# A gated-MLP down projection rewritten as Strassen's product of halves, partly run between the tiles of the up projection

## The chip, the cores and the metric

One core of a Trainium2 chip runs one program. The metric is the time on the device in microseconds (us), the median of several executions. The engines are TensorE (PE: matmuls into PSUM), VectorE (DVE), ScalarE (ACT), GpSimd (POOL) and SyncE (SP), which here issues the loads. PSUM has eight banks of 128 partitions x 512 fp32.

## The reference, cut to what matters

A diffusion block: adaLN, a token mixer with four branches, then a gated MLP with a depthwise convolution, and a final RMSNorm. 512 tokens, D = 1024 channels, hidden width F = 2816. Only the last part is changed:

```python
def conv_ffn(h, p):
    u, g = jnp.split(h @ p['ffn_w_up'], 2, axis=-1)
    g = depthwise_conv(g, p['ffn_conv_w'], p['ffn_conv_b'])
    return (jax.nn.silu(g) * u) @ p['ffn_w_down']
...
x = x + gate2 * conv_ffn(ada_norm(x, norm2_g, shift2, scale2), p)
return rmsnorm(x, final_norm_g)
```

## The kernel before

All matmuls keep about fp32 precision by splitting each operand into a rounded part and a rest: `hi` is a ScalarE cast to fp32r, `lo` a VectorE subtraction, and a product is three matmuls (hi·hi, hi·lo, lo·hi; helper `mm3`). So each weight tile that is loaded costs a ScalarE pass and a VectorE pass over it (`load_split`, tags "wh" and "wl" with three slots each, "wr" with two for the raw data).

Activations are channel-major: partitions are channels, the 512 tokens lie along the free dimension. The up projection makes 44 tiles (22 of gates g, 22 of u) of 8 x 3 = 24 matmuls each, with weights stationary and 512 tokens moving (`up`, L1015). For hidden tile f the loop at L1032 makes g, convolves it (one ScalarE pass, two VectorE passes out of PSUM), applies silu, makes u, multiplies, and splits the result into `act[f]`. The down projection (L1045) then makes eight output tiles of 128 channels, each over 22 hidden chunks, the last one in two halves of 256 tokens; each tile gets the gate and the residual, its squares are added up, it is transposed on TensorE and copied to token-major `xo`. The last tile is followed by the square root, the scaling of all rows and the four output transfers.

A scheduler orders the instructions of each engine once, at build time; each engine then runs its list in order and waits on semaphores. Every operation goes through one helper, so all carry line L60; names of tiles tell them apart. In PSUM four banks have the tag "big" (up tiles `pup`, down tiles `pdn`, and others) and four the tag "ps".

Of the kernel before, what the change touches and what calls it, by code (L numbers as in the profile page):

```python
# [8 lines left out]
F32 = mybir.dt.float32  # L9
F32R = mybir.dt.float32r  # L10
AF = mybir.ActivationFunctionType
ALU = mybir.AluOpType
# [6 lines left out]
KT = 8  # L19
# [2 lines left out]
EPS = 1e-6  # L22
FH = 2816
NF = FH // P
GW = 64
RW = 63

# [12 lines left out]
INV2PI = 1.0 / (2 * math.pi)  # L40
MAGIC = 1.5 * 2.0 ** 23
PI_LO = 3.1415925
CUT = 576


@with_exitstack
def block_kernel(ctx: ExitStack, tc: tile.TileContext, A):
# [24 lines left out]
    pp = ctx.enter_context(tc.tile_pool(name="psum", bufs=1, space=bass.MemoryType.PSUM))  # L72

    def ps(name="ps"):
        big = name in ("pin", "pbr", "pup", "pdn", "pwo", "pkc", "pvc")
        return pp.tile([P, T], F32, name=name, tag="big" if big else "ps", bufs=4)


# [37 lines left out]
    def col(name, i=0, n=1):  # L116
        o = COLS[name][0] + i
        return cols[:, o:o + n]
# [4 lines left out]
    def temp(pool, tag="hm"):  # L123
        return lambda n: pool.tile([P, T], F32, name="hm", tag=tag, bufs=2)[:, :n]
# [54 lines left out]
    hxh = hp.tile([P, KT, T], F32R, name="hxh")  # L179
    hxl = hp.tile([P, KT, T], F32R, name="hxl")  # L180

    def yslot(name, shape=(P, 2, T), dt=F32R):
        return hp.tile(list(shape), dt, name=name, tag="y", bufs=8)
# [812 lines left out]
    with ExitStack() as ff:  # L996
        fp = ff.enter_context(tc.tile_pool(name="ffn", bufs=1))
        h2h, h2l = hxh, hxl

        def tmp(n):  # L1000
            return yslot("hm", dt=F32)[:, 0, :n]

        for h, hs in enumerate(halves):
            if h:
                norm2_cols(h)
                norm2_rows(h)
            for k in range(KT):
                modulate(tmp, h2h[:, k, hs], h2l[:, k, hs], xt[k][:, hs], rb2[h], a2col[:, k:k + 1], modc[:, 8 + k:9 + k])
        act = []
# [12 lines left out]

        first = {}
        for m in (NF, 0, NF + 1):
            first[m] = (load_split(A["wup"][m], name="wup"), ps("pup"))
        for hs in halves:
            for ms in ((NF, 0), (NF + 1,)):
                for k in range(KT):
                    for m in ms:
                        up_step(first[m][1], first[m][0], k, hs)  # L1030

        for f in range(NF):  # L1032
            pg = first[NF + f][1] if NF + f in first else up(NF + f)
            gt = fp.tile([P, T], F32, name="gt", tag="gt", bufs=2)
# [4 lines left out]
            act.append(yslot("act") if f < 8 else fp.tile([P, 2, T], F32R, name="act", tag=f"act{f}"))  # L1039
            split(act[f][:, 0], act[f][:, 1], gt)  # L1040


        xo = fp.tile([P, 4, D], F32, name="xo")
        tmp = temp(fp)
        for mt in range(KT):  # L1045
            ws = []
            for c in range(0, NF, KT):
                n = min(KT, NF - c)
                ws.append(load_split(A["wdn"][mt, :, c * P:(c + n) * P], n * P, name="wdn"))
            for hs in ((full,) if mt < KT - 1 else halves):  # L1050
                p = ps("pdn")[:, hs]
# [4 lines left out]
                V.scalar_tensor_tensor(xt[mt][:, hs], p, modc[:, 24 + mt:25 + mt], xt[mt][:, hs], ALU.mult, ALU.add)  # L1056
                n = hs.stop - hs.start
                if mt < KT - 1:
                    sumsq(tmp, ssq[:, hs], xt[mt][:, hs], mt == 0)
                else:  # L1060
                    sq = tmp(n)
                    S.activation(sq, xt[mt][:, hs], AF.Square)
                xg = fp.tile([P, T], F32, name="xg", tag="gt", bufs=2)[:, hs]
                V.tensor_scalar(xg, xt[mt][:, hs], col("final", mt), None, ALU.mult)
                tt = range(4)[hs.start // P:hs.stop // P]
                if mt == KT - 1:
                    r = rms_cols(sum_cols(ssq[:, hs], sq))
                pt = ps("pxt")[:, hs]
                for i in range(len(tt)):
                    PE.transpose(pt[:, i * P:(i + 1) * P], xg[:, i * P:(i + 1) * P], ident)  # L1070
                if mt == 4:
                    preload_sqrt(ssq[:, 0:1])
                if mt < KT - 1:
                    S.copy(xo[:, tt.start:tt.stop, mt * P:(mt + 1) * P], pt.rearrange("p (t c) -> p t c", c=P))
                    continue
                for i, t in enumerate(tt):
                    rt = r[:, i:i + 1]
                    V.tensor_scalar(xo[:, t, :CUT], xo[:, t, :CUT], rt, None, ALU.mult)
                    S.mul(xo[:, t, CUT:mt * P], xo[:, t, CUT:mt * P], rt)
# [55 lines left out]
def _arrays(x, c, ctx, c_ctx, w_mod, b_mod, norm1_g, norm2_g, w_in, pool_w, pool_scale,  # L1135
# [78 lines left out]
```

## Time and profile before

| | |
|---|---|
| median of 3 runs | 856.35 us (856.13 to 857.44) |
| profiled execution, its own time | 855.23 us |
| its span in the trace | 853.4 us |
| TensorE busy | 832.1 us, 97% of the span |
| VectorE busy | 502.6 us, 59% |
| ScalarE busy | 332.1 us, 39% |
| up projection, first to last tile | about 475.6 to 717.8 us |
| down projection | 717.8 to 843.4 us |
| after the last matmul of the down projection | about 10 us |

Busy shares are averages over stages; what a stage is bound by is read from its own stretch. Matmul rows overlap their neighbours, so their durations can't be added up; the distance between starts counts.

### The profile page before, as it was taken

The page shows a single profiled execution, that of the slowest core. Times are in us where ns is not written, and L with a number is a line of the kernel's source. Part 1 is how long each engine was busy: PE and PEld are TensorE (multiplying, and loading weights), DVE is VectorE, ACT ScalarE, POOL GpSimd, SP SyncE. Part 2 cuts the span into 40 slices and gives each one's busy share as a digit, 9 for nine tenths or more (in the row PEclk, how much of TensorE's full clock was granted, in tenths as well). Part 3 has the DMA queues.
Part 4 walks back from the last instruction along what each step waited for, and adds up shares of the span by engine and source line. Part 5 has one row for each costly group of instructions (what it writes and reads, how often), then busy time and mean ns, then how long its engine had stood idle before and what let it go on. Part 6 is the DMA issues. An engine that isn't in the chain of part 4 may idle for free.

```text
span 853.4 us, 10736 instructions
## 1 busy us (share of the span) xinstructions
PE 832.1 (97%) x4192; PEld 683.8 (80%) x4192; DVE 502.6 (59%) x874; ACT 332.1 (39%) x519; POOL 5.9 (1%) x16
## 2 busy tenths in 40 slices
PE   6999999989999999999999999999999999999995
PEld 2577888868888888888889988888888888888885
DVE  4879998699797863445444964444444444232333
ACT  6634452625454332323333453333333333222321
POOL 0100000000000000000000000000000000000000
PEclk9999999999999999999999999999999999999998
DMA  8912314645656542223332233222222333332312
GB/s 315 414 60 74 99 44 140 190 144 208 210 166 220 185 158 93 93 93 130 113 122 76 74 124 99 98 97 92 91 96 95 99 99 93 87 107 84 93 57 99
DMA packets 30363, 107.31 MB, mean 126 GB/s; under 512 B 3783, under 2 KB 4935, under 8 KB 29288
## 3 DMA queue, kind: packets, MB, share of 16 engines
q1 hardware_dynamic: 30312, 106.62, 37.6%
q8 instruction: 33, 0.54, 0.3%
q14 instruction: 18, 0.15, 0.0%
HBM read 104.51 MB, written 2.10 MB: 125 GB/s over the span
## 4 chain that ended last, share of the span: by engine, by line
PE 86%; DVE 8%; ACT 2%; DMA 1%; issue 1%; SPq 0%; DVEq 0%; ACTq 0%
PE pup L60 28%; PE pin L60 25%; PE pdn L60 14%; PE pwo L60 5%; PE pbr L60 5%; PE pss L60 1%; DVE za L60 1%; PE pKe L60 1%; PE pav L60 1%; DVE winl L60 1%; DVE zb L60 1%; PE pmod L60 1%; DMA cb<-in_crow_dram 1%; DMA wm<-in_wmB_dram 1%; DVE wgl L60 1%
## 5 line engine op out<-in xcount | busy, mean ns | idle before, releaser
L60 PE MATMUL pup<-hxh,wupl 128*128 128x512 f32 (+1 forms) x376 | 140.8, 376 | 0.0
L60 PE MATMUL pup<-hxl,wuph 128*128 128x512 f32 (+1 forms) x376 | 140.6, 376 | 0.0
L60 PE MATMUL pup<-hxh,wuph 128*128 128x512 f32 (+1 forms) x376 | 139.9, 376 | 0.7 <-ACT wuph L60 0.4
L60 PE MATMUL pdn<-act,wdnh 128*128 128x512 f32 (+1 forms) x396 | 112.7, 368 | 0.0
L60 PE MATMUL pin<-hxh,wgh 128*128 128x512 f32 x256 | 101.2, 395 | 0.6 <-ACT wgh L60 0.6
L60 PE MATMUL pin<-hxh,wgl 128*128 128x512 f32 x256 | 100.3, 392 | 0.0
L60 PE MATMUL pin<-hxl,wgh 128*128 128x512 f32 x256 | 100.2, 391 | 0.0
L60 DVE TENSOR_TENSOR wupl<-wupr,wuph 128x1024 fp32r<-128x1024 f32 x44 | 53.9, 1225 | 71.7 <-ACT wuph L60 69.8
L60 ACT CAST wuph<-wupr 128x1024 fp32r<-128x1024 f32 x44 | 46.3, 1053 | 92.6 <-PE pup L60 90.2
L60 PEld LDWEIGHTS pdn<-act,wdnh 128*128 128x128 f32 x396 | 71.6, 189 | 12.0
L60 PEld LDWEIGHTS pup<-hxh,wupl 128*128 128x128 f32 x376 | 70.7, 188 | 13.1 <-DVE wupl L60 0.2
L60 PEld LDWEIGHTS pup<-hxh,wuph 128*128 128x128 f32 x376 | 70.1, 188 | 13.7 <-ACT wuph L60 0.6
L60 PEld LDWEIGHTS pup<-hxl,wuph 128*128 128x128 f32 x376 | 70.6, 188 | 12.8
L60 PE MATMUL pdn<-act,wdnl 128*128 128x512 f32 (+1 forms) x198 | 72.4, 366 | 0.0
L60 DVE TENSOR_TENSOR wdnl<-wdnr,wdnh 128x1024 fp32r<-128x1024 f32 (+1 forms) x24 | 27.2, 1134 | 63.3 <-ACT wdnh L60 63.2
L60 ACT ACTIVATE sg<-pin 128x512 f32<-128x512 f32 x32 | 19.2, 600 | 113.5 <-PE pin L60 113.4
L60 DVE SCALAR_TENSOR_TENSOR sg<-sg,pbr 128x512 f32<-128x512 f32 x24 | 16.5, 689 | 75.8 <-PE pbr L60 75.8
L60 PEld LDWEIGHTS pin<-hxh,wgh 128*128 128x128 f32 x256 | 48.1, 188 | 10.5 <-ACT wgh L60 1.0
L60 PEld LDWEIGHTS pin<-hxh,wgl 128*128 128x128 f32 x256 | 48.1, 188 | 10.3 <-issue 0.5
L60 PEld LDWEIGHTS pin<-hxl,wgh 128*128 128x128 f32 x256 | 48.1, 188 | 9.8 <-issue 0.5
L60 ACT CAST wdnh<-wdnr 128x1024 fp32r<-128x1024 f32 (+1 forms) x24 | 23.6, 983 | 72.5 <-PE pdn L60 66.7
L60 PE MATMUL pin<-hxh,winh 128*128 128x512 f32 x128 | 51.7, 404 | 0.0
(265 smaller groups left out, 1427.5 us busy)
## 6 DMA issues: line engine op xcount, KB each, us to landing
wupr<-in_wup_dram SPq DMA_DIRECT2D x44, 512.0 KB, 3.4
wgr<-in_wg_dram SPq DMA_DIRECT2D x32, 640.0 KB, 3.9
wm<-in_wmB_dram SPq DMA_DIRECT2D x32, 512.0 KB, 4.6
wm<-in_wmA_dram SPq DMA_DIRECT2D x8, 1024.0 KB, 9.9
winr<-in_win_dram SPq DMA_DIRECT2D x16, 512.0 KB, 3.5
wdnr<-in_wdn_dram SPq DMA_DIRECT2D x16, 512.0 KB, 3.5
wor<-in_wout_dram SPq DMA_DIRECT2D x8, 512.0 KB, 3.5
wdnr<-in_wdn_dram SPq DMA_DIRECT2D x8, 384.0 KB, 3.1
```

Of the source, the lines that this page charges most:

```text
L60: ins = f(*a, **k)
```

## The change

The down projection becomes Strassen's product. Its operands are halved: tokens 0-255 and 256-511, hidden channels 0-1407 and 1408-2815 (NH = 11 chunks each), output channels 0-511 and 512-1023. Seven products of halves take the place of eight; each has 11 chunks x 2 blocks of 128 tokens x 3 terms. Activations are now stationary (128 x 128) and weights move (512 columns), so results come out token-major. Sums of activation halves are made by VectorE (`pair`), sums of weight halves by accumulating loads that GpSimd issues onto a buffer `rsum` (W11, then W12 added, and so on). Three products (`part`: banks pb1, pb3, pb2) get one chunk at a time, put between the up tiles; of the other four, p2 and p3 load plain weights and p7 and p4 take the sums in `rsum`; before p4, `t4_load` adds W11 and W21 to each chunk of `rsum` once p7 has split it. The residual is transposed to token-major before the fourth up tile instead of after each down tile. The gate becomes a row `g2b` (eight small matmuls), and all residual adds, squares and scalings run on token-major rows. Hidden tiles come in pairs (f, f + 11). The hx tiles are cut in halves.

```diff
-        for f in range(NF):
+        def part(j, k):
+            r = rsum[:, k]
+            if j == 0:
+                nc.sync.dma_start(r, A["wdq"][0, 0, :, k])
+            else:
+                nc.gpsimd.dma_start(r, A["wdq"][j - 1, 1, :, k], accum_op=ALU.add)
+            w = wsplit(r)
...
+            if j == 2:
+                nc.sync.dma_start(r, A["wdq"][0, 1, :, k])
+                nc.gpsimd.dma_start(r, A["wdq"][1, 1, :, k], accum_op=ALU.add)
+            prod((pb1, pb3, pb2)[j], tps[k][:, j, 0], tps[k][:, j, 1], w, k)
+
+        def run_part(keep=2):
+            if len(todo) > keep:
+                part(*todo.pop(0))
...
+        def hidden(f):
             pg = first[NF + f][1] if NF + f in first else up(NF + f)
...
             S.activation(gt, gt, AF.Silu)
+            run_part()
             pu = first[f][1] if f in first else up(f)
             V.tensor_mul(gt, gt, pu)
...
-        for mt in range(KT):
...
-                for k in range(NF):
-                    wh, wl = ws[k // KT]
-                    w = slice((k % KT) * P, (k % KT + 1) * P)
-                    mm3(p, wh[:, w], wl[:, w], act[k][:, 0, hs], act[k][:, 1, hs], k == 0, k == NF - 1)
...
+        for k in range(NH):
+            hidden(k)
+            half_pair(k)
+            run_part()
+            hidden(NH + k)
+            pair(k)
+            if k < NH - 1:
+                run_part()
+        while todo:
+            run_part(0)
...
+        def product(x, raws, tail=0, then={}):
+            b = [ps("pda") for _ in range(2)]
+            late = []
+            for c, ks in enumerate(chunks):
+                hi, lo = wsplit(raws(ks))
+                for f in then.get(c, ()):
+                    f()
...
+        def t4_load(ks):
+            for i in range(2):
+                nc.gpsimd.dma_start(rs(ks), A["wdq"][i, 0, :, ks[0]:ks[-1] + 1], accum_op=ALU.add)
...
+        p2 = product(lambda k: (a2s[k][:, 0, :TC], a2s[k][:, 1, :TC]), w21, then=then)
+        then = {c: [call(t4_load, ks)] for c, ks in enumerate(chunks)}
...
+        p7 = product(lambda k: s34k(0, k), rs, then=then)
...
+        p4 = product(lambda k: (a2s[k][:, 0, TC:], a2s[k][:, 1, TC:]), rs, then=then)
+        p3 = product(lambda k: s34k(1, k), w22, 3, then={1: [call(y21, 0)], 2: [call(y21, 1)]})
...
+        V.tensor_mul(ms[1], p3[1], g2b[:, hi_])
+        V.tensor_add(xo[:, 1, hi_], xo[:, 1, hi_], ms[1])
+        rstd_b(0)
+        sumsq2(1, 1)
+        last_scale(0)
+        rstd_a(1, 1)
+        rstd_b(1)
+        last_scale(1)
```

How the change moves instructions is seen at three places. The first is VectorE's list where the last up tile ends. Before, one product and one split stand there, then only weight splits (wdnl):

```order
L60 TENSOR_TENSOR gt<-gt,pup 128x512
L60 TENSOR_TENSOR wdnl<-wdnr,wdnh 128x768
L60 TENSOR_TENSOR act<-gt,act 128x512
L60 TENSOR_TENSOR wdnl<-wdnr,wdnh 128x1024 x2
L60 SCALAR_TENSOR_TENSOR x_3656<-pdn,modc,x_3656 128x512
```

After, from behind the product with the last up tile to the split of the last part's weights (s_6267: the activation sums s1; tp: their lo parts; a_6277: the split of g2; s_6345: splits for p7; dg: a diagonal for the gate row):

```order
L60 TENSOR_TENSOR wdnl<-rsum,wdnh 128x512
L60 TENSOR_TENSOR s_6267<-gt 128x256
L60 TENSOR_TENSOR a_6277<-gt,a_6277 128x512
L60 TENSOR_TENSOR tp<-s_6267,tp 128x256
L60 TENSOR_TENSOR s_6267<-s_6267,gt 128x256
L60 TENSOR_TENSOR s_6345<-sc,s_6345 128x256
L60 TENSOR_TENSOR sc<-s_6267,gt 128x256
L60 TENSOR_TENSOR s_6345<-sc,s_6345 128x256
L60 TENSOR_TENSOR tp<-s_6267,tp 128x256
L60 TENSOR_TENSOR s_6345<-sc,s_6345 128x256 x2
L60 TENSOR_SCALAR dg<-ident,modc 128x128
L60 TENSOR_TENSOR wdnl<-rsum,wdnh 128x512
```

The weight split of the last part has moved behind sums and splits of activations. The second place is VectorE's list in the products at the end. Before, in each down tile, three weight splits stand beside three passes of 512 columns:

```order
L60 TENSOR_TENSOR wdnl<-wdnr,wdnh 128x1024 x2
L60 SCALAR_TENSOR_TENSOR x_3694<-pdn,modc,x_3694 128x512
L60 TENSOR_TENSOR wdnl<-wdnr,wdnh 128x768
L60 TENSOR_TENSOR ssq<-ssq,hm 128x512
L60 TENSOR_SCALAR xg<-x_3694,cols 128x512
```

After, inside p4 (pda here is the finished p7; vv and u_6334 are sums of products, m a gated result, s_6676 splits for p3):

```order
L60 TENSOR_TENSOR vv<-vv,pda 128x512
L60 TENSOR_TENSOR wdnl<-rsum,wdnh 128x1024
L60 TENSOR_TENSOR u_6334<-u_6334,pda 128x512
L60 TENSOR_TENSOR m<-vv,g2f 128x512
L60 TENSOR_TENSOR wdnl<-rsum,wdnh 128x1024
L60 TENSOR_TENSOR xo<-xo,m 128x512
L60 TENSOR_TENSOR s_6676<-sc,s_6676 128x256
L60 TENSOR_TENSOR vv<-vv,pda 128x512
L60 TENSOR_TENSOR u_6334<-u_6334,pda 128x512
L60 TENSOR_TENSOR m<-vv,g2f 128x512
L60 TENSOR_TENSOR wdnl<-rsum,wdnh 128x1024
```

Between two weight splits there are now up to five other passes. The third place is GpSimd's list, which held no loads before; its last ones are now those for p4 (DMASW: the landing of an earlier load of GpSimd, DVE: p7's split of the chunk):

```order
L1200 DMA rsum<-in_wdq_dram 128x1024 [waits DMASW1_49,DVE_49]
L1200 DMA rsum<-in_wdq_dram 128x1024 [waits DMASW2_49,DMASW1_49]
L1200 DMA rsum<-in_wdq_dram 128x1024 [waits DVE_49]
L1200 DMA rsum<-in_wdq_dram 128x1024 [waits DMASW4_49,DVE_49]
L1200 DMA rsum<-in_wdq_dram 128x1024 [waits DMASW5_49,DVE_49]
L1200 DMA rsum<-in_wdq_dram 128x1024 [waits DMASW3_49]
L1200 DMA rsum<-in_wdq_dram 128x1024 [waits DMASW7_49,DMASW4_49]
L1200 DMA rsum<-in_wdq_dram 128x1024 [waits DMASW5_49,DMASW0_49]
L1200 DMA rsum<-in_wdq_dram 128x1024 [waits DVE_49]
L1200 DMA rsum<-in_wdq_dram 128x512 [waits DMASW2_49,DVE_49]
L1200 DMA rsum<-in_wdq_dram 128x1024 [waits DMASW1_49]
L1200 DMA rsum<-in_wdq_dram 128x512 [waits DMASW2_49]
```

The first load of chunks 1 to 3 is issued before the second load of chunk 1; chunks 4 and 5 follow.

## Rows read from the trace of the kernel before

**Rows 1.** The page: span, and each engine's busy us, share and instructions.

```profile
span 853.4 us, 10736 instructions
...
PE 832.1 (97%) x4192; PEld 683.8 (80%) x4192; DVE 502.6 (59%) x874; ACT 332.1 (39%) x519; POOL 5.9 (1%) x16
```

**Rows 2.** By stretch: busy us of each engine (instructions), granted clock, DMA share, GB/s.

```profile
493.00:717.80 224.80, 224.80 (x1001) 186.49 (x1001) 110.46 (x129) 86.67 (x109) 0.00 (x0) 1.00 0.31 100
717.80:843.40 125.60, 125.60 (x636) 106.30 (x634) 40.34 (x56) 33.78 (x43) 0.00 (x0) 1.00 0.29 85
843.40:853.40 10.00, 1.24 (x11) 0.99 (x9) 3.28 (x12) 1.64 (x4) 0.00 (x0) 0.73 0.27 106
```

**Rows 3.** What TensorE waited for, 476 to 845 us: total, times, longest.

```profile
PE pxt L60 <- DVE xg L60: 0.9, 1, 0.9
PE pup L60 <- ACT wuph L60: 0.4, 1, 0.4
```

**Rows 4.** Timeline of TensorE: start, us, form, count (512 and 256 columns, transposes).

```profile
818.36 0.62 PE L60 MATMUL pdn<-act,wdnh 128*128 128x512 f32 x2
...
819.04 0.62 PE L60 MATMUL pdn<-act,wdnh 128*128 128x512 f32 x2
...
826.91 0.40 PE L60 MATMUL pdn<-act,wdnh 128*128 128x256 f32 x2
...
827.27 0.40 PE L60 MATMUL pdn<-act,wdnh 128*128 128x256 f32 x2
...
828.59 0.28 PE L60 MATMUL pdn<-act,wdnl 128*128 128x256 f32 x1
...
828.80 0.63 PE L60 MATMUL pxt<-ident,xg 128*128 128x128 f32 x4
...
829.18 0.48 PE L60 MATMUL pdn<-act,wdnh 128*128 128x256 f32 x2
```

**Rows 5.** Groups of 717.8 to 853.4 us by form: count, busy us, mean ns, idle before.

```profile
L60 PE MATMUL pdn<-act,wdnl 128*128 128x512 f32 x154 | 59.9, 389 | 0.0
...
L60 DVE TENSOR_TENSOR wdnl<-wdnr,wdnh 128x1024 fp32r<-128x1024 f32 x14 | 17.2, 1225 | 59.6 <-ACT wdnh L60 59.6
...
L60 ACT CAST wdnh<-wdnr 128x1024 fp32r<-128x1024 f32 x14 | 14.7, 1053 | 45.8 <-PE pdn L60 45.8
L60 PE MATMUL pdn<-act,wdnl 128*128 128x256 f32 x44 | 12.4, 283 | 0.0
...
L60 DVE TENSOR_TENSOR ssq<-ssq,hm 128x512 f32<-128x512 f32 x6 | 4.1, 685 | 0.0
L60 ACT ACTIVATE hm<-x 128x512 f32<-128x512 f32 x6 | 3.8, 636 | 1.0 <-DVE x L60 0.9
```

**Rows 6.** Timeline of VectorE: passes in sequence, the next pair's, a 256-column add.

```profile
539.60 1.23 DVE L60 TENSOR_TENSOR wupl<-wupr,wuph 128x1024 fp32r<-128x1024 f32 x1 [3.61 <-ACT wuph L60]
540.74 1.53 DVE L60 SCALAR_TENSOR_TENSOR gt<-pup,cols,gt 128x511 f32<-128x511 f32 x2
...
550.48 1.23 DVE L60 TENSOR_TENSOR wupl<-wupr,wuph 128x1024 fp32r<-128x1024 f32 x1 [3.61 <-ACT wuph L60]
...
471.30 0.42 DVE L60 TENSOR_TENSOR ssq<-ssq,hm 128x256 f32<-128x256 f32 x1
```

**Rows 7.** DMA: a stretch near the start, and the page's one data queue, one issue.

```profile
21.00:43.00 22.00, 21.64 (x158) 12.47 (x158) 18.45 (x43) 13.26 (x25) 3.83 (x3) 1.00 1.01 415
...
q1 hardware_dynamic: 30312, 106.62, 37.6%
...
wupr<-in_wup_dram SPq DMA_DIRECT2D x44, 512.0 KB, 3.4
```

**Rows 8.** Timeline of the end: last matmul's followers, last write, output transfers.

```profile
838.70 10.04 SPq L1081 DMA_DIRECT2D out_dram<-xo  x4
...
843.33 0.28 PE L60 MATMUL pst<-ones,ssq 128*128 128x1 f32 x2
...
847.99 0.35 DVE L60 TENSOR_SCALAR xo<-pxt,rr 128x128 f32<-128x128 f32 x1
```

More of the change, by code (lines that the diff above doesn't have):

```diff
@@ L74, in ps @@
     def ps(name="ps"):
[L75 removed]
+        big = name in ("pin", "pbr", "pup", "pdn", "pwo", "pkc", "pvc", "pgb")
         return pp.tile([P, T], F32, name=name, tag="big" if big else "ps", bufs=4)
@@ L1030, in block_kernel @@
                         up_step(first[m][1], first[m][0], k, hs)
-        for f in range(NF):
+        for mt in range(KT):
+            pt = ps("pxt")
+            for i in range(4):
+                PE.transpose(pt[:, i * P:(i + 1) * P], xt[mt][:, i * P:(i + 1) * P], ident)
+            S.copy(xo[:, :, mt * P:(mt + 1) * P], pt.rearrange("p (t c) -> p t c", c=P))
+        rsum = fp.tile([P, NH, T], F32, name="rsum")
+        pb1, pb2, pb3 = [], [], []
+        a2s, s34, tps = [], [], []
+        todo = []
@@ new lines, in prod, with wsplit @@
+        def prod(b, ah, al, w, k, tts=(0, 1)):
+            for t in tts:
+                c = slice(t * P, (t + 1) * P)
+                PE.matmul(b[t], ah[:, c], w[0], start=k == 0, stop=False)
+                PE.matmul(b[t], ah[:, c], w[1], start=False, stop=False)
+                PE.matmul(b[t], al[:, c], w[0], start=False, stop=k == NH - 1)
+        def wsplit(raw):
+            n = raw.shape[-1]
+            hi = wp.tile([P, WCH], F32R, name="wdnh", tag="wh")[:, :n]
+            lo = wp.tile([P, WCH], F32R, name="wdnl", tag="wl")[:, :n]
+            split(hi, lo, raw)
+            return hi, lo
@@ new lines, in block_kernel @@
+        for k in range(NH):
[8 more added lines that the diff above has]
+            run_part(0)
+        g2f = hp.tile([P, 2, D], F32, name="g2f", tag="hx0")
+        g2b, gfb = g2f[:, 0], g2f[:, 1]
+        nc.sync.dma_start(gfb, A["finrow"].broadcast_to([P, D]))
+        e1 = fp.tile([P, 2, T], F32, name="e1", tag="tp", bufs=2)
+        for t in range(2):
+            S.copy(e1[:, t], pb1[t])
@@ new lines, in wraw @@
+        def wraw(i, j, ks):
+            raw = wp.tile([P, WCH], F32, name="wdnr", tag="wr", bufs=2)[:, :len(ks) * T]
+            nc.sync.dma_start(raw, A["wdq"][i, j, :, ks[0]:ks[-1] + 1])
+            return raw
+        chunks = [list(range(c, min(c + 2, NH))) for c in range(0, NH, 2)]
+        def product(x, raws, tail=0, then={}):
[5 more added lines that the diff above has]
+                    f()
+                for i, k in enumerate(ks):
+                    w = hi[:, i * T:(i + 1) * T], lo[:, i * T:(i + 1) * T]
+                    if c < len(chunks) - tail:
+                        prod(b, *x(k), w, k)
+                    else:
+                        late.append((w, k))
+            for t in range(2):
+                for w, k in late:
+                    prod(b, *x(k), w, k, (t,))
+            return b
@@ new lines, in g2_row, with s34_split @@
+        def g2_row(h):
+            pb = ps("pgb")
+            for i in range(4):
+                mt = 4 * h + i
+                dg = cp.tile([P, P], F32, name="dg", tag="dg", bufs=2)
+                V.tensor_scalar(dg, ident, modc[:, 24 + mt:25 + mt], None, ALU.mult)
+                PE.matmul(pb[:, i * P:(i + 1) * P], ones, dg, start=True, stop=True)
+            S.copy(g2b[:, h * T:(h + 1) * T], pb)
+        s34s = [[], []]
+        def s34_split(j, ks):
+            cs = slice(j * TC, (j + 1) * TC)
+            for k in ks:
+                if k % 4 == 0:
+                    s34s[j].append(hp.tile([P, 4, 2, TC], F32R, name="s34", tag=f"hx{1 + k // 4}"))
+                split(s34s[j][-1][:, k % 4, 0], s34s[j][-1][:, k % 4, 1], s34[k][:, cs])
@@ new lines, in scale_low, with call @@
+        def scale_low(t):
+            V.tensor_mul(xo[:, t, lo_], xo[:, t, lo_], gfb[:, lo_])
+        def call(f, *a):
+            return lambda: f(*a)
+        then = {c: [call(s34_split, 0, ks)] for c, ks in enumerate(chunks)}
+        for t in range(2):
+            then[1 + t].append(call(uv, t))
+            then[3 + t].append(call(g2_row, t))
+        p2 = product(lambda k: (a2s[k][:, 0, :TC], a2s[k][:, 1, :TC]), w21, then=then)
+        then = {c: [call(t4_load, ks)] for c, ks in enumerate(chunks)}
@@ new lines, in block_kernel @@
+        ms = []
+        for t in range(2):
+            ms.append(fp.tile([P, T], F32, name="ml", tag="vv", bufs=2))
+        V.tensor_mul(ms[0], p3[0], g2b[:, hi_])
+        V.tensor_add(xo[:, 0, hi_], xo[:, 0, hi_], ms[0])
+        sumsq2(0, 1)
+        rstd_a(0, 1)
+        V.tensor_mul(ms[1], p3[1], g2b[:, hi_])
[6 more added lines that the diff above has]
+        last_scale(1)
```

155 lines of the change are left out of this document (111 added, 44 removed).

## The prediction

> **What bounds the kernel now.** I read the page first. TensorE is busy 97% of the 853.4 us span, VectorE 59% [rows 1]. An average proves nothing about one stage, so I split the end of the kernel: from 493.0 to 717.8 us (up projection) and from 717.8 to 843.4 us (down projection) TensorE is busy the whole of each stretch at a granted clock of 1.00, the upper level (2.4 GHz), while VectorE has 110.46 of 224.8 us and 40.34 of 125.6 us, and ScalarE less [rows 2]. The list of TensorE's waits from 476 to 845 us has two entries, 0.4 us at the first up tiles and 0.9 us in the tail [rows 3]. So here only TensorE's instruction stream sets the time, and a matmul taken out shortens the kernel by its spacing, until something else becomes late.
>
> The spacing is read from starts, because a row's duration (389 ns) overlaps its neighbours. Three 512-column matmuls pass from 818.36 to 819.04 us, so one takes 0.227 us; three 256-column ones pass from 826.91 to 827.27 us, so one takes 0.120 us; an up pair is 48 of the former in 10.88 us (539.60 to 550.48 us between the same splits on VectorE [rows 6]), again 0.227; four transposes with the matmuls around them fill 828.59 to 829.18 us, of which one matmul is 0.12, so about 0.12 us a transpose [rows 4].
>
> **The change, part by part.** *Matmuls.* Before, the down projection has 22 chunks x 3 terms = 66 matmuls per tile: seven tiles of 512 columns and the last in two halves (154 and 44 rows of the term with wdnl, a third of all) [rows 5]. That is 462 x 0.227 + 132 x 0.120 = 104.9 + 15.8 us. After, seven products of 11 chunks x 2 token blocks x 3 terms are 7 x 66 = 462 matmuls of 512 columns, again 104.9 us (15.0 us a product). Removed: **15.8 us**. The 32 transposes are still there, only in front of the fourth up tile. There they need a ScalarE copy each four; eight copies lie beside the first tiles, with nothing due for 5 us. Eight 128-column matmuls make the gate row (1.0 us at a transpose's price); sixteen one-column sums go away, which overlap their neighbours (843.33, two in 0.28 us [rows 8]). I take **+0.3**.
>
> *Three products in the up stage.* 29 of their 33 parts stand between up tiles, each 6 matmuls = 1.36 us. PSUM: the up tiles keep two of the four "big" banks, so a tile's bank must be read within the next tile (5.44 us); its readers, one ScalarE pass and two VectorE passes of 0.75 us, need under 3. Weight buffers: three slots now serve tiles and parts, so a slot is split again when the third matmul group back ends, and the result is due one tile and one part (6.8 us) later; the chain is a 1.05 us cast and a 1.23 us subtraction. Per pair of hidden tiles VectorE has 4 x 1.23 (up splits), 3 x 0.69 (part splits), 4 x 0.75, 2 x 0.69 + 0.69 and 7 x 0.42 = 15.0 us in 4 x 5.44 + 3 x 1.36 = 25.8 us [rows 5, 6]. I cost the insertion at nothing: the cover is 4 us of slack at each split. If that cover fails by 0.5 us a time, it costs 29 x 0.5 = 14.5 us. The accumulating loads of a part have about 10 us from the split of the part before on the same slot; SP's reload stands behind two or three weight loads that are already due, and on GpSimd only other loads wait behind it. A 512 KB plain load lands in 3.4 us [rows 7], so even one three times as slow is covered there.
>
> *End of the up stage.* VectorE's order shows fourteen instructions between the last tile's end and the split that the last part needs: four of 512, nine of 256, one of 128 columns. At 0.69 and 0.42 us, less about 0.09 us where the next one is independent (1.14 us from start to start of a 1.23 us one [rows 6]), that is 5.6 to 6.8 us. TensorE has three parts left to cover it, 4.1 us. Then the first 1024-column split of the next product needs 1.9 us more against 1.4 us. I take **+2.3** (bounds 1 to 4).
>
> *Four products at the end.* In the rows of p7, p4 and p3, VectorE has 17 instructions of 1024 columns, 29 of 512, 11 of 256 and a dozen of one column: 17 x 1.225 + 29 x 0.685 + 11 x 0.42 + 2 = 47.3 us by duration, near 43 us by spacing, against 3 x 15.0 = 45 us of TensorE. Before, the same engine was at a third in this stage [rows 2]. It becomes as loaded as TensorE, runs in order, and the weight subtractions stand between residual adds that wait for a finished product. Walking p4 by these prices, the fourth chunk's subtraction ends about 0.5 us after TensorE wants it; in p2 the third is 0.7 us late; in p3, behind two 1024-column multiplies, the fifth and sixth are 1 to 1.5 us late each. What is late is then TensorE's next lo matmul. Together **+3.5** (bounds 0, if spacing is tighter, to 7).
>
> *The loads for p4 (T4).* They are twelve accumulating loads from GpSimd, eleven of which carry a half-megabyte in effect (5.77 MB), each chunk's second behind the landing of its first, and all in one order. The trace of before has no accumulating load, nor any issued by GpSimd (all its data go through one queue, q1, that SP feeds [rows 7]). Counted from p7's start, the first can go 1.6 us earlier (its chunk's split frees the buffer), p4 starts at 15.0 and must have its fifth chunk by about 23.5 us. As bounds by near rows: if it runs as the plain loads at their best, 415 GB/s with all engines busy [rows 7], the bytes need 14 us and TensorE never waits: 0. If reading the old contents beside the new halves that to 207 GB/s, a load takes 2.5 us on the engines, the second load of the second chunk lands 17 us after p7's start (2 us late), the second of the fifth at 29 (3 us late after that shift), and 1 MB of p3's weights, which SP sends at the same time, adds 2.5 us: 7.5 us, of which VectorE wins back 2.5 since it catches up meanwhile. The value in between, as neither row is nearer, is **+2.8**.
>
> *Tail.* Before, 4.9 us pass from the last matmul to the last VectorE write and 5.1 more to the span's end, with the output transfer [rows 8]. After it: two 512-column passes (0.69 each), a square (0.64), seven one-column steps at 0.2, the first block's scaling (0.75), its own (0.69) and five hand-overs of 0.1 are 5.4 us, while the first block's output starts earlier. **+0.4**.
>
> A rule that speaks against the T4 loads: the Trainium skill, "Collectives: The Full Stack", section "The bandwidth ceiling: the fold count and why AG ≠ RS ≠ AR", says that a reducing transfer runs at half the rate of a copying one, because it reads two sources through one ring. By that rule T4 would cost the upper bound above instead of 2.8, and the sum would come out some 2 us higher; no run shown here has such a transfer.
>
> **Sum.** -15.8 + 0.3 + 2.3 + 3.5 + 2.8 + 0.4 = -6.5. The profiled execution took 855.23 us (853.4 of span and 1.8 around it), so 848.7; the median of the three runs, 856.35, lies 1.1 above it: **849.8 us**. About 0.2% (1.7 us) is what a measurement of this kernel tells from no change.
>
> **Rivals.**
> *Accumulating loads at half rate* (as bounded above): the terms become -15.8 + 0.3 + 2.3 + 1 + 7.5 + 0.4 = -4.3, so 852 us, up to 855 if their fixed part is longer than a plain load's. This is what the Trainium skill's rule above would give. For: two streams are read; against: the bytes before use 85 GB/s of 415 here [rows 2, 7]. Chance 0.2.
> *T4 loads far slower, the side of the loss.* If an accumulating load moves r GB/s, the last chunk is there 5770/r us after p7 starts at -1.6, plus 2 for latency, and is wanted by 26.5. The gain without T4, with VectorE's lateness hidden, is some 11 to 12 us, used up when the loads end at 38 us: near r = 150. At 100 it costs 32 us: 876 us. Pauses of that length also bring the clock down: in the last 10 us, where TensorE is busy 1.24 us, the granted clock is 0.73 on average [rows 2], so p3 could run partly at 1.2 GHz. Against: nothing in the trace moves so slowly in large rows. Chance 0.16.
> *The inserted parts stall the up stage*, 0.3 to 0.7 us at each of 29: -15.8 + 9.3 (the other terms above) + 9 to 20, so 859 to 870 us. For: two PSUM banks in place of four, three slots shared. Against: TensorE waited for a split once, for 0.4 us, and half of VectorE is free [rows 2, 3]. Chance 0.08.
> *No lateness at all*: VectorE keeps up and T4 lands in time: -15.8 + 0.3 + 1.5 + 0.4, 843 to 845.5 us. Chance 0.08.
> That the change doesn't remove the matmuls is excluded: the order of its TensorE rows has 462 wide ones in the place of 594.
>
> **How the numbers follow.** The forecast's own range is 845.5 to 852 (VectorE 0 to 7, T4 0 to 5), chance 0.48. The range is 843 to 863: it leaves out the worse part of the T4 rival (0.10), half of the stalled up stage (0.04) and a little of the lower end (0.03). Faster by over 0.2% (below 854.6): 0.48 + 0.08 + 0.16 of the half-rate case = 0.72. Within 0.2%: 0.08, the upper end of the half rate and the least part of the two losing rivals. Slower: 0.20.
>
> **What would show it.** Right: the up stage with 29 parts lasts 39.4 + 3.8 us longer (parts and transposes) with TensorE busy throughout; a pause of 2 to 3 us after the last up tile, ended by VectorE's split; 60 us of four products with VectorE above 90% and short waits of TensorE for wdnl; T4 loads that land in about 4 us. Wrong: in p4 TensorE, VectorE and ScalarE idle together until a load on the software queue lands, each of more than 6 us; or, in the up stage, waits for the lo or hi split at every inserted part; or a granted clock below 1.00 in p4 or p3.

## The result, and the profile after

The changed kernel takes **862.33 us** (median) beside 856.57 us of the kernel before on the same chip: ratio 1.0057 over all executions of both (1.0067 for the two medians), 95% interval 1.0043 to 1.0072, so **0.6% slower**. The forecast was 849.8 us and faster; the measured time is inside its range and on the other side of no change. The execution that was profiled is the one of 862.33 us.

The head of its page: span, then busy us of each engine, share of the span, instructions.

```profile
span 860.5 us, 10855 instructions
...
PE 824.4 (96%) x4060; PEld 671.9 (78%) x4060; DVE 560.5 (65%) x1021; ACT 367.2 (43%) x610; POOL 45.1 (5%) x61
```

Against [rows 1], TensorE's busy time went down and the span went up, so TensorE now waits or runs slower. The group of the up tiles' matmuls (duration min/median/max, first and last start) says that this isn't in the up stage:

```profile
L60 PE MATMUL pup<-hx,wuph x752: 278/389/476, 476.4 to 761.5; 128*128 128x512 f32 x164, 128*128 128x256 f32 x24
```

The up tiles' last matmul starts at 761.71 us; the last product matmul starts at 851.01. The list of TensorE's waits from 470 us on (waiting row and what ended the wait: us in total, times, longest) and the 10 us windows (busy us and instructions of each engine, then granted clock, DMA share, GB/s) have it all behind that point, as [rows 3] and [rows 2] had nothing there:

```profile
PE pda L60 <- ACT wdnh L60: 9.3, 3, 5.0
PE pdn L60 <- ACT tp L60: 2.6, 1, 2.6
PE pda L60 <- DVE wdnl L60: 1.4, 3, 0.8
```

```profile
760.00:770.00 10.00, 6.92 (x32) 5.23 (x30) 6.06 (x16) 5.59 (x16) 0.86 (x1) 1.00 0.53 108
770.00:780.00 10.00, 8.35 (x31) 6.86 (x32) 8.29 (x16) 4.46 (x6) 0.86 (x1) 0.83 0.57 151
...
800.00:810.00 10.00, 9.48 (x42) 7.51 (x40) 7.03 (x14) 4.51 (x9) 2.05 (x3) 1.00 1.05 204
810.00:820.00 10.00, 5.03 (x11) 3.66 (x12) 5.35 (x8) 4.54 (x8) 2.32 (x3) 0.68 1.03 198
820.00:830.00 10.00, 7.09 (x29) 5.29 (x29) 5.12 (x9) 2.69 (x7) 1.73 (x2) 0.98 0.52 84
830.00:840.00 10.00, 10.00 (x39) 8.06 (x38) 7.69 (x14) 3.51 (x5) 0.00 (x0) 0.83 0.37 107
```

Two places lose time: just behind the last up tile (760 to 780), and p4 (810 to 830). In p4's windows VectorE and ScalarE are about as idle as TensorE. From 800 to 820 the DMA engines are full (share 1.03 to 1.05) and yet move only 198 to 204 GB/s; from 820 to 830 they are half empty (0.52). Each place is followed by a stretch with a granted clock below 1.00.

What ended the waits is in the chain that ended last (start, us, what):

```profile
758.17 6.78 DMA rsum<-in_wdq_dram
...
765.02 0.63 ACT wdnh L60
...
765.67 0.70 DVE wdnl L60
...
766.66 0.86 POOL rsum L1080
...
789.91 5.69 DMA rsum<-in_wdq_dram
...
797.50 11.65 DMA rsum<-in_wdq_dram
...
810.22 10.63 DMA rsum<-in_wdq_dram
...
821.13 6.00 DMA rsum<-in_wdq_dram
```

All of these transfers are accumulating loads. At the first place the load for the part (1, 10) lands 6.78 us after its issue began, ScalarE casts its weights, VectorE subtracts, and only then GpSimd issues the load for the part (2, 10) into the same buffer. ScalarE runs in order, so operands (tp) that need no load are late as well; its two casts of rsum there and their idle time:

```profile
765.02 0.62 ACT L60 CAST wdnh<-rsum 128x512 fp32r<-128x512 f32 x1 [3.98 <-DMA rsum<-in_wdq_dram]
...
770.98 0.62 ACT L60 CAST wdnh<-rsum 128x512 fp32r<-128x512 f32 x1 [1.41 <-DMA rsum<-in_wdq_dram]
```

In p4 the same engine stands idle 8.41 and 7.10 us for T4's loads, the longest of which takes 11.65 us:

```profile
813.41 1.04 ACT L60 CAST wdnh<-rsum 128x1024 fp32r<-128x1024 f32 x1 [8.41 <-DMA rsum<-in_wdq_dram]
...
827.24 1.04 ACT L60 CAST wdnh<-rsum 128x1024 fp32r<-128x1024 f32 x1 [7.10 <-DMA rsum<-in_wdq_dram]
```

The timeline of TensorE in p4 shows what follows a wait (start, us; xN are N matmuls in one row):

```profile
814.51 0.80 PE L60 MATMUL pda<-wdnh,a 128*128 128x512 f32 x1 [5.03 <-ACT wdnh L60]
...
816.37 1.05 PE L60 MATMUL pda<-wdnh,a 128*128 128x512 f32 x2
817.22 0.63 PE L60 MATMUL pda<-wdnl,a 128*128 128x512 f32 x1
817.64 1.05 PE L60 MATMUL pda<-wdnh,a 128*128 128x512 f32 x2
...
821.02 0.62 PE L60 MATMUL pda<-wdnh,a 128*128 128x512 f32 x2
821.48 0.40 PE L60 MATMUL pda<-wdnl,a 128*128 128x512 f32 x1
821.71 0.62 PE L60 MATMUL pda<-wdnh,a 128*128 128x512 f32 x2
```

Three matmuls take 1.27 us (816.37 to 817.64) behind the 5.03 us wait and 0.69 us (821.02 to 821.71) later: the lower and the upper of the two clock levels.

**The theory** that the experiments test: accumulating loads move some 200 GB/s at most, half of what copying loads do. T4's 5.77 MB then need near 29 us where p7 lasts 15, and at the end of the up stage, where parts follow one another with no up tile between, two such loads lie bare. **The rivals**: VectorE's load in the four products (a term of 3.5 us in the forecast); GpSimd's queue, in order, with each chunk's second load behind the landing of its first, whatever the transfers do; and VectorE's fourteen instructions at the end of the up stage (a term of 2.3).

### The profile page after: what moved, and what is told of

Read it like the earlier page. It is cut to its first block, busy times and chain, and to the rows that moved or that the text cites. A ratio compares the mean times of both kernels' runs of the same rounds, so it can differ in the third digit from the quotient of the medians.

```text
span 860.5 us, 10855 instructions
## 1 busy us (share of the span) xinstructions
PE 824.4 (96%) x4060; PEld 671.9 (78%) x4060; DVE 560.5 (65%) x1021; ACT 367.2 (43%) x610; POOL 45.1 (5%) x61
## 5 line engine op out<-in xcount | busy, mean ns | idle before, releaser
L60 PE MATMUL pup<-hx,wuph 128*128 128x512 f32 (+1 forms) x752 | 219.9, 376 | 0.7 <-ACT wuph L60 0.4
L60 PE MATMUL pin<-hx,wgh 128*128 128x512 f32 x512 | 160.7, 393 | 0.6 <-ACT wgh L60 0.6
L60 PEld LDWEIGHTS pup<-hx,wuph 128*128 128x128 f32 x752 | 138.1, 188 | 26.5 <-ACT wuph L60 0.6
L60 PE MATMUL pup<-hx,wupl 128*128 128x512 f32 (+1 forms) x376 | 140.8, 376 | 0.0
L60 PEld LDWEIGHTS pin<-hx,wgh 128*128 128x128 f32 x512 | 95.0, 188 | 20.3 <-ACT wgh L60 1.0
L60 PE MATMUL pin<-hx,wgl 128*128 128x512 f32 x256 | 100.3, 392 | 0.0
L60 PE MATMUL pin<-hx,winh 128*128 128x512 f32 x256 | 81.5, 398 | 0.0
L60 PEld LDWEIGHTS pup<-hx,wupl 128*128 128x128 f32 x376 | 70.7, 188 | 13.1 <-DVE wupl L60 0.2
L60 ACT CAST wuph<-wupr 128x1024 fp32r<-128x1024 f32 x44 | 46.3, 1053 | 80.5 <-PE pup L60 75.1
L60 ACT CAST wdnh<-rsum 128x512 fp32r<-128x512 f32 (+1 forms) x45 | 32.3, 718 | 74.1 <-PE pup L60 44.1
L60 PEld LDWEIGHTS pin<-hx,wgl 128*128 128x128 f32 x256 | 48.1, 188 | 10.3 <-issue 0.5
L60 PE MATMUL pin<-hx,winl 128*128 128x512 f32 x128 | 50.5, 395 | 0.2 <-DVE winl L60 0.2
L60 DVE TENSOR_TENSOR gt<-gt,pup 128x512 f32<-128x512 f32 x22 | 15.1, 687 | 52.1 <-PE pup L60 47.9
L60 DVE CUSTOM_DVE_ANT_0 wm<-wm,cb 128x1024 f32<-128x1024 f32 x32 | 38.7, 1216 | 13.3 <-ACT cb L60 8.2
## 6 DMA issues: line engine op xcount, KB each, us to landing
wm<-in_wmA_dram SPq DMA_DIRECT2D x8, 1024.0 KB, 10.2
```

Of the source, the lines that this page charges most:

```text
L60: ins = f(*a, **k)
```

## The experiments

The start of the up stage differs among the profiled executions (476.2 to 478.7 us in the kernels with the change), so the stretch from the last up matmul to the last product matmul is compared, by their starts in each timeline. "Waits" is the sum of TensorE's waits there, "rest" the stretch without them: a remainder, not a measurement of its own. The experiments ran on four chips, and each ratio to before is taken on one, so a gain by medians and one by ratios can differ.

| kernel | last up, last product (us) | stretch | waits | rest |
|---|---|---|---|---|
| the change | 761.71, 851.01 | 89.3 | 13.3 | 76.0 |
| T4 by copying loads | 762.40, 836.62 | 74.2 | 4.8 | 69.4 |
| T4 by one load a chunk | 761.46, 836.57 | 75.1 | 4.3 | 70.8 |
| last k unsummed | 761.63, 843.65 | 82.0 | 9.1 | 72.9 |
| copying T4 and last k unsummed | 763.94, 833.70 | 69.8 | 1.2 | 68.6 |
| p7 ahead of p2 | 761.92, 844.71 | 82.8 | 7.8 | 75.0 |
| p2 between the last parts | 762.81, 848.83 | 86.0 | 11.6 | 74.4 |
| p2 split around p7 | 763.30, 840.25 | 77.0 | 5.0 | 72.0 |
| p2 and p7 mixed | 762.08, 841.28 | 79.2 | 6.3 | 72.9 |
| T4 summed in the up stage | 763.97, 834.98 | 71.0 | 2.0 | 69.0 |
| the same, gain on GpSimd | 762.19, 836.27 | 74.1 | 4.4 | 69.7 |

### T4 by copying loads

```diff
-    nc.gpsimd.dma_start(rs(ks), A["wdq"][i, 0, :, ks[0]:ks[-1] + 1], accum_op=ALU.add)
+    nc.gpsimd.dma_start(rs(ks), A["wdq"][i, 0, :, ks[0]:ks[-1] + 1])
```

> The ten loads of T4 stay on GpSimd's queue, with their tiles, sizes and order, but copy in place of adding, so p4 multiplies by W21 alone and half of y21 is not the layer's. Theory (adding loads run at about half the rate of copying ones, and p4 waits for them): TensorE's waits of 5.03, 0.46, 2.15 and 0.76 us in p4 shrink to under 2 us in sum, and the slow clock behind them with them: 851, within 849 to 853.5. Rival A (the order and the issue on GpSimd's queue, each second load behind the first one's landing, not the adding): the waits stay, 859 or more. Rival B (VectorE's load in the four products): 861 to 863.

Measured 847.56 us, ratio to before 0.9905 (0.989 to 0.9921): 14.8 us less than the change by the medians, 13.0 by the ratios: more than expected. The queue, its order and the landings that each second load waits for stay; only the adding is gone, and p4's waits with it. Of the 15.1 us that the stretch falls by, 13.9 lie behind p7's first matmul (59.4 us to the last product in the change, 45.4 here); the rest lies ahead of any T4 load and can't be theirs. The DMA view of the two kernels shows the rate itself (forty slices of equal length; tenths of the engines' time, then GB/s). First the change, 789 to 830 us:

```profile
DMA  6887970097999999999999999999993129899500
GB/s 92 340 148 112 208 156 0 0 80 132 204 200 204 212 216 212 204 216 200 200 188 196 192 200 196 212 216 200 208 186 56 22 20 88 164 206 192 98 0 0
```

Then this kernel, 789 to 812 us:

```profile
DMA  5487885210009699999999798898999987210056
GB/s 100 185 321 235 249 299 235 114 57 0 0 0 135 214 420 406 427 420 413 420 435 385 207 378 349 214 299 349 370 349 356 378 342 306 100 71 7 0 100 121
```

With the engines full, adding moves 186 to 216 GB/s (but for the slice in which it starts, 80) and copying up to 435. Rivals A and B both fall as the cause by themselves. Whether the order and the landings add to the wait while the loads are slow is another question, to which this run has no answer.

### T4 by one adding load a chunk

```diff
-    for i in range(2):
+    for i in range(1):
         nc.gpsimd.dma_start(rs(ks), A["wdq"][i, 0, :, ...], accum_op=ALU.add)
```

> One adding load for each chunk of T4 in place of two (W11 alone is added, W21 left out, so half of y21 is not the layer's): 2.9 MB in place of 5.8 MB. Theory of the adding rate (about 200 GB/s): 2.9 MB take some 14 us, p7 lasts 15, so p4's waits go to under 1.5 us: 851.5, within 849.5 to 854. Rival (queue order and latency of a load, not bytes): each chunk still waits a landing of some 6 to 11 us behind its issue, 856 to 859.

Measured 847.73 us, ratio 0.991 (0.9893 to 0.9926): below the expected interval. Half the adding bytes are worth as much as copying them all, as it should be if bytes against p7's 15 us decide. But this edit also takes away each second load's wait for a landing, so by itself it doesn't tell the two apart.

### The last k without its adding loads

```diff
-    else:
+    elif k < NH - 1:
         nc.gpsimd.dma_start(r, A["wdq"][j - 1, 1, :, k], accum_op=ALU.add)
```

> The last k's two parts (j 1 and 2 of k 10) multiply by what the buffer holds, without their adding loads; their share of the products is not the layer's. Theory (the two adding loads are bare at the end of the up stage, since the parts there follow one another with no up tile between): TensorE's 2.62 and 2.11 us there go to under 1.5 us in sum and the clock of 770 to 780 stays higher: 856, within 854.5 to 858. Rival (VectorE's fourteen instructions and ScalarE's casts behind the last up tile, the forecast's own term): they still take some 2.3 us there, 860 to 862.

Measured 853.31 us, ratio 0.9969 (0.9958 to 0.9979): 9.0 us less than the change by the medians, 7.5 by the ratios, and more than expected; the stretch has 7.3 of it. TensorE waits for nothing between the last up tile and p2 (busy 10.00 us of 760 to 770). The 1.4 us that it still waits ahead of p7 are those of a matmul of the gate row inside p2, behind a plain load of W21 for which ScalarE waits 2.79 us (775.46). So two adding loads were the wait. In the change itself, too, VectorE stands idle in front of the last part's split, until a cast that waits for a load:

```profile
771.63 0.69 DVE L60 TENSOR_TENSOR wdnl<-rsum,wdnh 128x512 fp32r<-128x512 f32 x1 [1.25 <-ACT wdnh L60]
```

That VectorE's fourteen instructions would cost nothing is not shown, though: with the loads gone the scheduler moved five of them behind that split, which now ends at 766.27 us, 0.28 ahead of the matmul that needs it.

### Both together

> The copying loads of T4 and the last k without its adding loads, in one kernel (both leave out part of the layer's sums, as in the two kernels before). Theory (adding loads at these two places cost all that the forecast lacks): the two gains add, 847.6 less the 9.0 that the end gave: 838.6, within 837 to 841.5. Rival (VectorE as loaded as TensorE, and its fourteen instructions behind the last up tile: 3.5 + 2.3 us of the forecast): 843 to 846.

Measured 843.57 us, ratio 0.9849 (0.9835 to 0.9864), which is in the rival's interval, but not by its mechanism. The theory's sum lies 5 us lower. By the ratios, which compare on one chip, the gains are 13.0, 7.5 and 17.8 us, so only 2.7 are lacking; in the stretch the two gains overlap by 2.9 (15.1 + 7.3, but 19.5 together), which would account for that. The profiled execution also began the up stage 2.3 us later than that of the change (478.7 against 476.4); whether the others did isn't known. Waits and windows of this kernel:

```profile
PE pgb L60 <- DVE dg L60: 1.2, 1, 1.2
```

```profile
790.00:800.00 10.00, 10.00 (x46) 8.29 (x45) 10.00 (x15) 7.17 (x14) 4.21 (x8) 1.00 0.80 275
800.00:810.00 10.00, 10.00 (x46) 8.28 (x45) 10.00 (x18) 7.16 (x14) 1.61 (x3) 1.00 0.70 251
810.00:820.00 10.00, 10.00 (x46) 8.29 (x45) 8.65 (x15) 3.74 (x6) 0.00 (x0) 1.00 0.17 53
```

VectorE is busy for the whole of 790 to 810, and TensorE doesn't wait. p7, p4 and p3 pass from 788.33 to 833.93 us, 45.6 us for 3 x 15.0, so VectorE, whose order in these products is that of the change, costs at most 0.6 us there in place of 3.5, and the rival falls. p2 takes 18.55 us (769.78 to 788.33): 15.0, the 1.2 us wait, and some 2.3 for the gate row, whose eight matmuls show as sixteen rows, where the forecast had 1.0. This "rest" of 68.6 us is the floor for the table. What the other kernels have above it, **7.4 us in the change beside 13.3 us of waits**, is put down mostly to the lower clock (0.83, 0.68 and 0.83 in three of the change's windows above); it wasn't measured apart.

### The loads by themselves

Only loads, in phases that follow one another (the first adding load starts beside the last copying ones): eight of 512 KB copied by SP's queue, eight copied by GpSimd's, eight added by GpSimd's, then single ones of 256 KB, three of each.

> No layer at all: 512 KB loads of the down weights by themselves, eight at a time, copied by SP's queue, copied by GpSimd's queue, added by GpSimd's queue, and then single 256 KB ones of the three kinds. Theory: copying at about 400 GB/s by either queue, adding at about 200 GB/s (half), 16 DMA engines full in both. Rival A (GpSimd's queue is slow whatever it does): copying on it at 200 to 250 GB/s too. Rival B (adding is not slower, only late): adding at 350 GB/s or more.

The page's slices (2.25 us each; the page's last part gives KB each and median us from issue to landing):

```profile
POOL 0000008940003994000000021120302202000000
DMA  2999952999999699999999915333343032144233
GB/s 40 346 426 417 409 226 36 364 386 402 382 302 213 95 204 204 211 215 209 255 277 280 322 69 60 56 49 67 36 80 93 24 116 55 62 116 116 70 156 124
```

This kernel ran once. With the engines at 9: copying 346 to 426 GB/s by SP, 364 to 402 by GpSimd (then 302 and 213, as the first adding load runs beside), adding 204 to 215 (the 255 to 322 behind it has an output transfer beside). A single 256 KB load, from the issue on GpSimd to VectorE's read, is 4.2 us when it adds and 3.1 when it copies, and GpSimd is held 0.87 and 0.55 us. Rivals A and B fall. The Trainium skill, "Collectives: The Full Stack", section "The bandwidth ceiling: the fold count and why AG ≠ RS ≠ AR", puts a reduce-scatter between cores, whose add reads two sources, at half the rate of an all-gather, which copies; for these loads, 204 to 215 beside up to 426 GB/s agrees.

### p7 ahead of p2

```diff
+p7 = product(lambda k: s34k(0, k), rs, then=then)        # T4's loads start here
 p2 = product(lambda k: (a2s[k][:, 0, :TC], a2s[k][:, 1, :TC]), w21, then=then)
-p7 = product(lambda k: s34k(0, k), rs, then=then)
```

> The same arithmetic with p7 ahead of p2: T4's adding loads start as each chunk of p7 has been split and have p2's 15 us more. Theory of the adding rate: 5.8 MB at about 200 GB/s take 29 us, p7 and p2 last 30, so p4 waits under 2 us: 852, within 850 to 854.5. Rival A (p2's plain W21 loads run beside them and come late by as much, so that the wait moves to p2): 856 to 860. Rival B (p7's first weights are there, but its split operands are not, and the end of the up stage grows): TensorE waits 2 to 4 us more there, 855 to 858.

In this kernel the final gain multiplies two half rows of the output ahead of the sum that it should follow: the same instructions, another result. Measured 855.81 us, ratio 0.9997 (0.9986 to 1.0007): just below rival A's interval and inside rival B's, but at the end of the up stage TensorE waits 2.7 us where the change waits 4.7, so rival B falls. p4 no longer waits for wdnh; p2 does, as rival A has it. ScalarE's casts of W21's chunks:

```profile
796.83 1.04 ACT L60 CAST wdnh<-wdnr 128x1024 fp32r<-128x1024 f32 x1 [5.05 <-DMA wdnr<-in_wdq_dram]
...
806.83 1.05 ACT L60 CAST wdnh<-wdnr 128x1024 fp32r<-128x1024 f32 x1 [4.40 <-DMA wdnr<-in_wdq_dram]
```

With the DMA engines full (share 1.04 to 1.05 from 780 to 810) the lateness moved to plain loads.

### p2 between the last parts

```diff
-while todo:
-    run_part(0)
+run_part(0); run_part(0)
 ...
+p2_run(0, 1)
+run_part(0)
+p2_run(2)
+run_part(0)
```

> The layer's full arithmetic: p2's first two chunks stand ahead of the part (1, 10) and its third ahead of the part (2, 10), with p2's sums in the banks that the last up tiles leave. Theory (two bare adding loads): p2's 5.4 and 2.7 us of matmuls cover them, as leaving them out did: 853.5, within 852 to 855.5, with p4's waits as they were. Rival (VectorE's and ScalarE's queue of the end is the wait): the first chunk of p2 waits for its split instead, 857 or more.

Measured 858.91 us, ratio 1.0023 (1.001 to 1.0036): less than half of the expected gain, and in the rival's interval, but without its mechanism: 760 to 770 is full, so the first chunk of p2 doesn't wait for its split, but the second load is issued only when the part (1, 10) has been split, and the part (2, 10) still waits 1.68 us; p4's waits stay (5.96 and 2.19 us in front of wdnh).

### p2 split around p7, and p2 and p7 mixed

In both, p2's first chunks stand between the last parts, then comes p7, then p2's rest, then p4. The second puts four chunks of p2 and one of p7 ahead of the part (2, 10); the diff leads from the first to the second.

```diff
-p2_run(2)
+p2_run(2, 3)
+p7_run(0)
 run_part(0)
-p7 = product(...)
-p2_run(3, 4, 5)
+p7_run(1, 2, 3, 4, 5)
+p2_run(4, 5)
```

> The layer's full arithmetic: p2's first three chunks between the last parts as in the kernel before, then p7, then the rest of p2, then p4. T4's adding loads start with p7, 23 us ahead of p4 in place of 15, and only three chunks of W21 are loaded beside them. Theory: 5.8 MB at some 200 GB/s are done some 29 us behind p7's start, each chunk just ahead of its split: 841, within 838.5 to 844.5. Rival A (the plain loads share the DMA engines and come late, as they did with p7 ahead of the whole of p2): 845 to 850. Rival B (the products now hold more VectorE work than TensorE's): 846 or more with TensorE waiting for wdnl.

> The layer's full arithmetic, as with p2 split before, but four chunks of p2 and one of p7 stand ahead of the part (2, 10) and every W21 chunk is on its way ahead of T4's adding loads, which begin with p7's second chunk. Theory: the 1.67 us in front of the part (2, 10) and W21's lateness (5.1 us of ScalarE waiting for its last chunk) go; T4 still needs some 29 us and is done at the last splits of p4: 847, within 844 to 850. Rival (the adding loads take all DMA engines whatever stands beside them, so p4's last chunks and p3's first W22 chunks come late): 851 to 855, with TensorE waiting in p4 for wdnh or wdnl.

Measured 852.84 us, ratio 0.9958 (0.9942 to 0.9975), and 853.5 us, ratio 0.997 (0.9956 to 0.9984): both faster than before, and the second no better than the first. The first lies above rival A's interval and in the open one of rival B, and shows marks of both: ScalarE waits 5.10 us for a chunk of W21 (803.48), and TensorE 2.8 us for wdnl. The second lies in its rival's interval. In the second the end of the up stage is full and W21 is early, but T4's loads still end late: ScalarE waits 4.95 us in front of p4's first cast (803.06) and 7.28 in front of a later one (816.43). Its DMA share is 1.05 to 1.06 from 790 to 810. A wider stretch for the same 5.77 MB wins some of the loss back, and no more.

### T4 summed in the up stage

Fewer adding bytes, together with another order. The part of j 2 ends with W11 + W12 + W22 in its buffer, so one adding load of W21 makes T4 of it, in the up stage. p4 comes ahead of p7, and p7's W12 + W22 is then one copying and one adding load a chunk, in place of two adding ones behind the up stage.

```diff
 if j == 2:
-    nc.sync.dma_start(r, A["wdq"][0, 1, :, k])
-    nc.gpsimd.dma_start(r, A["wdq"][1, 1, :, k], accum_op=ALU.add)
+    nc.gpsimd.dma_start(r, A["wdq"][1, 0, :, k], accum_op=ALU.add)
...
+def t7_load(ks):
+    nc.sync.dma_start(rs(ks), A["wdq"][0, 1, :, ks[0]:ks[-1] + 1])
+    nc.gpsimd.dma_start(rs(ks), A["wdq"][1, 1, :, ks[0]:ks[-1] + 1], accum_op=ALU.add)
...
+p2_run(0, 1); run_part(0); p2_run(2, 3)
+p4_run(0); run_part(0); p4_run(1, 2, 3, 4, 5)
+p2_run(4, 5)
+p7 = product(...)
```

> The layer's full arithmetic with fewer adding loads behind the up stage: the part of j 2 is followed by one adding load of W21, which makes T4 of its sum (in place of a reload and an adding load); p4 comes ahead of p7, and p7's W12+W22 is made by one copying and one adding load a chunk while p4 and the rest of p2 run; four chunks of p2 and one of p4 stand ahead of the part (2, 10). Theory: 2.9 MB at some 200 and 2.9 MB at some 400 GB/s, 21 us of the DMA engines where p4 and p2's rest give 19 and p7's own pace the rest, so TensorE waits under 2 us in sum: 843.5, within 841 to 847. Rival (VectorE: y11, y21 and y22 now all stand in p7 and p3, with the last splits): 847 to 851, with waits for wdnl in p3 and a later end of the tail.

Measured **846.61 us, ratio to before 0.9888** (0.987 to 0.9907): 1.1% faster than before, at the layer's full arithmetic and with the same matmuls as the change; it is inside the theory's interval, near its upper end. What the fewer bytes and what the order contribute was not separated. Its waits behind the up stage, in one row, and two windows:

```profile
PE pda L60 <- DVE wdnl L60: 2.0, 3, 1.1
```

```profile
790.00:800.00 10.00, 10.00 (x52) 8.26 (x51) 6.35 (x14) 3.90 (x5) 3.83 (x5) 1.00 1.03 254
800.00:810.00 10.00, 10.00 (x46) 8.23 (x45) 9.98 (x15) 6.13 (x10) 0.00 (x0) 1.00 0.82 197
```

The DMA engines are still full from 790 to 800, but nothing is late, and the clock stays at 1.00. What is left are waits for VectorE in p3, as the rival has them.

### The final gain on GpSimd

```diff
-V.tensor_mul(xo[:, t], xo[:, t], gfb)
+G.tensor_tensor(xo[:, t], xo[:, t], gfb, ALU.mult)
```

> The kernel with T4 summed in the up stage, with the final norm's gain (two multiplies of 512 and two of 1024 columns) on GpSimd in place of VectorE; the layer's full arithmetic. Theory (with the adding loads out of the way VectorE, busy 9.3 to 10 of 10 us from 800 to 830, is what TensorE's last 1.4 us of waits come from): VectorE is relieved of 3.8 us, the waits for wdnl go: 845.2, within 844 to 846.2. Rival (GpSimd takes several times VectorE's 1.22 us for 1024 columns, and the first output rows wait for it): 847.5 to 851.

Measured 847.85 us, ratio 0.99 (0.9884 to 0.9917): no gain over the kernel above, whose interval it overlaps, and in the rival's interval. GpSimd needs 3.15 to 3.17 us for the 1024 columns that take VectorE 1.21:

```profile
822.98 3.17 POOL L60 TENSOR_TENSOR xo<-xo,g2f 128x1024 f32<-128x1024 f32 x1 [10.85 <-ACT m L60]
830.33 3.15 POOL L60 TENSOR_TENSOR xo<-xo,g2f 128x1024 f32<-128x1024 f32 x1 [4.17 <-ACT m L60]
```

TensorE's waits for wdnl grew to 4.4 us, and the trace shows where: a weight split that VectorE begins while GpSimd multiplies takes longer. One of 1024 columns (824.78) takes 2.45 us in place of 1.22, one of 512 (831.2) 2.87 in place of 0.69; each ends 0.5 to 1.1 us behind GpSimd's multiply, and TensorE waits 1.11 us (827.29) and 1.13 us (834.08) for them. Why the multiply holds them up isn't shown; other passes of VectorE beside it keep their length (0.69 us at 823.20), and the order of VectorE's rows in p3 changed with the edit.

## Why the prediction was wrong

- **Matmuls removed, and parts in the up stage at nothing: right.** The up stage, first to last start of its matmuls with wuph, is 285.1 us (476.4 to 761.5), and 242.0 in the kernel before (475.6 to 717.6): 43.1 us longer where 29 parts and the transposes were to take 43.2, with TensorE busy throughout. The rival of the stalled up stage is out.
- **The T4 term failed: +2.8 was taken, 12 to 14 us is what the runs show** (from p7's first matmul to the last product the time falls by 13.9 us when T4's loads copy, and by 12.0 when they do so in the kernel without the last k's loads). The step put the value between copying at 415 GB/s and half of that, "as neither row is nearer". Half was the rate, and the half-rate rival's 7.5 us were still too few. That working set the loads end to end at 2.5 us each, and the trace shows them otherwise. The start was as forecast (first issue 789.91, p7's first matmul 791.64), but the load took 5.69 us, GpSimd issued nothing until it had landed, and the engines moved nothing for two of the slices above (some 795 to 797 us). Then four loads are issued within 1.6 us (795.89 to 797.50), share the rate, and land after 5.8, 7.8, 9.7 and 11.65 us. The second chunk needs the second of them and then its own second load (issued at 804.49, landed after 8.8 us), so it is cast at 813.41, 21.8 us behind p7's start in place of 17.

  From the first issue to the last landing (828.4) T4's loads take 38.5 us, some 10 more than 5.77 MB at 204 GB/s. How much of the wait is the rate's and how much the order's and the landings' stays open: no run kept the adding and changed these alone.

  And the forecast had the slow clock only in the rival of far slower loads; here it fell behind a wait of 5 us. That rival's mechanism, pauses and then p4 and p3 partly at 1.2 GHz, came at 200 GB/s already, not near 150, and with it the sign that the prediction names for being wrong: the three engines idle together until loads of GpSimd's queue land, of 6.0 to 11.65 us.
- **The end of the up stage failed in its cause.** +2.3 stood for VectorE's fourteen instructions. With the adding loads gone TensorE waits for nothing there; the loads cost 7.3 us of the stretch by themselves, and 4.5 once T4's are copying ones. Without the loads five of the fourteen had moved behind the split. By their spacing (four at 0.34 us, one at 0.2) they would have made it some 1.3 us late, which is an estimate: a part of the +2.3 may have been right, and hidden behind the loads. The step "about 10 us" of cover for a part's adding load holds between up tiles. It was carried over to the last k, whose three parts have none between them.
- **VectorE as loaded as TensorE: the load was right (10.00 of 10 us where the loads are not late), the lateness was not**: at most 0.6 us in three products in place of +3.5. In the kernel with T4 summed in the up stage, where p3 holds more of VectorE's adds, it is seen: 2.0 us of waits for wdnl.
- **The small terms.** The gate row is some 2.3 us where 1.0 was taken. From the last product matmul to the end of the span the change has 9.5 us (851.01 to 860.5), before 10.2 (843.20 to 853.4): -0.7 in place of +0.4.

The stretch adds up: 68.6 us for four parts, four products and the gate, 13.3 of waits and a remainder of 7.4, mostly slower matmuls, make the 89.3 measured. The forecast's own terms come to 65.4 + 1.0 + 2.3 + 3.5 + 2.8 = 75.0.

## What to carry to other kernels

A sum made by the loads is not free: count its bytes at the adding rate, against the time of the stage that hides it, and count what else those engines must load there. When a stage's cover is worked out per step, look at its last step apart, where the next step's cover is missing. And before a late load is moved, ask whether its bytes can be had from what the buffer already holds: here one load a chunk less, and copying in place of half the adding behind the up stage, came to 846.61 us with a new order, where new orders alone came to 852.84 and more.

## What the runs showed of the hardware

- Adding loads fill all 16 DMA engines at 204 to 215 GB/s; plain loads beside them come late (a W21 chunk held ScalarE up for 5.05 us).
- Loads in flight together share that rate: four adding loads of 512 KB issued within 1.6 us landed after 5.8 to 11.65 us, where one takes 2.5 at the full rate (0.52 MB / 207). That later chunks issued early delay the one that is due is argued from this; no run limited the loads in flight.
- An adding load by itself takes 4.2 us for 256 KB, a copying one of GpSimd's 3.1, from the issue to VectorE's read.
- Waits of 2.62 and 2.11 us close together were followed by a granted clock of 0.83 (770 to 780), one of 5.03 by 0.68 in its row; matmuls then took 1.27 us a three in place of 0.69. In the kernel that copies T4, waits of 2.1 and 1.9 us came with no row below 1.00.
- VectorE's weight splits that began beside a GpSimd multiply of 1024 columns took 2.45 and 2.87 us in place of 1.22 and 0.69.
